# Entrance of the experts: token weights, slot weights, activation table and unread products moved or dropped

## The chip, the cores and the metric

The kernel runs on one core of a Trainium2 chip. The core has five engines with queues of their own, which are worked off in the order written: TensorE (PE in the profile, its weight loads PEld), VectorE (DVE), ScalarE (ACT), GpSimd (POOL) and SyncE (SP), and 16 DMA engines. The metric is the time of one execution in microseconds (us), lower is better: 1363.2 us is the median of three runs (1360.3 to 1363.39).

## The reference

The program is an encoder trunk with two layers on 512 tokens of width 1024. Each layer has a mixer (two kinds of attention) and a mixture of 16 experts, of which every token uses two. What matters here is the second part:

```python
scores = jax.nn.sigmoid((t @ w_router).astype(jnp.float32))
sel = scores + router_bias.astype(jnp.float32)
...
_, idx = lax.top_k(jnp.where(in_group, sel, -jnp.inf), TOP_K)
top_s = jnp.take_along_axis(scores, idx, axis=-1)
gate = top_s / jnp.sum(top_s, -1, keepdims=True)
...
act = jax.nn.silu(hg) * hu * combine[..., None].astype(t.dtype)
y = jnp.einsum('tef,efd->td', act, w_down)
```

The router picks one of four groups of experts and two experts in it; `gate` is the weight of each chosen expert for a token, and an expert's hidden activation is multiplied by it.

## The kernel before, in words

Each expert has 128 slots (`CAP`). The kernel does not run every expert on every token: it computes for each slot of an expert the number of the token that sits there (`tidx`), gathers these rows of `h2d` from DRAM with an indirect DMA of GpSimd (`x_load`, tile `xe`), transposes them on TensorE (`x_split`, tile `tp`), and splits them into a high and a low part (`xH` by ScalarE, `xL` by VectorE). The weights of gate, up and a half of down are split in the same way: ScalarE casts 512 columns into `wH` (line 217), VectorE subtracts into `wL` (line 218); there are six buffers of each (`NWH`). A product is then three matmuls (lines 227 to 229): high by high, low by high, high by low. An expert takes 24 of them for gate (8 blocks of 128 channels), 24 for up, and 8 wider ones for down.

The stage between the router and the first expert, which is called the entrance here, runs once per layer:

- VectorE ranks the scores, and TensorE counts the places (`pos`, lines 1068 to 1071). VectorE turns places into eight one-hot tiles `ats` (line 1088), TensorE multiplies them into `mp` (line 1090), and VectorE reads `tidx` out of it (line 1100).
- Behind `mp` TensorE has seven products of 512 columns into `idle` (line 1096), which nothing reads.
- GpSimd gathers the rows of the first expert. Then every engine loads the largest count `cnti` (line 1229) and branches: if an expert had more than 128 tokens, a loop (`overflow`) would handle the rest. It is not taken with these inputs. Instructions written behind the branch cannot be issued ahead of it, and a buffer that the branch would use is only free when the engine that would use it has passed its own branch.
- Behind the branch come the casts and subtractions of expert 0's weights, the transposes of its rows, and its products. `token_weights` (lines 1106 to 1111: six small VectorE operations, with the copy `posf`) gives each token the weights of its two experts. `slot_weights` (lines 1117 to 1121) turns them to the order of slots: ScalarE converts `ats` to 32 bits (`atf`, 1024 columns), TensorE multiplies it with the weights (`gp`, eight products of 16 columns, two instructions each in the profile), VectorE copies `gp` to `gsl`. The first reader of `gsl` is the end of expert 0's up product (line 1166).
- ScalarE loads its table of functions twice here: at its first cast behind the branch (line 217) and at the first Silu (line 1159).

What order the engines work in is decided when the program is built: a scheduler places instructions by their dependences, and `tc.issue_after(z.ins)` holds instructions back behind the one named. Behind the entrance the experts run in a steady cycle, e + 1's rows being split while e's down product runs. Experts' weights come in by SyncE's DMA queue, 1 MB per transfer; the first seven are loaded ahead, five more wait for the first gather (`load_held`, a one-column ScalarE copy at line 1311).

Of the kernel before, what the change touches and what calls it, by code (L numbers as in the profile page):

```python
# [12 lines left out]
AF = mybir.ActivationFunctionType  # L13
# [5 lines left out]
P = 128  # L19
S = 512  # L20
D = 1024
NT = S // P
# [62 lines left out]
def build(tc, A, out):  # L85
    nc = tc.nc
    with ExitStack() as es:
# [11 lines left out]
        V, ACT, PE, PO, SY = nc.vector, nc.scalar, nc.tensor, nc.gpsimd, nc.sync  # L99

        def f4(name, shape, dt=F32):
            return fp.tile([P] + list(shape), dt, tag="f4", name=name)
# [4 lines left out]
        def sc(name, shape, dt=F32, p=P):  # L107
            return sp.tile([p] + list(shape), dt, tag="sc", name=name)

        def small(name, shape, dt=F32, bufs=4, p=P):  # L110
            return sm.tile([p] + list(shape), dt, tag=name, name=name, bufs=bufs)
# [4 lines left out]
        def ptp(shape, name="tp", dt=F32):  # L116
            return ps.tile(shape, dt, tag="tp", name=name, bufs=2)

        def pat(shape, name="at"):
            return ps.tile(shape, F32, tag="at", name=name, bufs=4)  # L120
# [19 lines left out]
        for n in ("ident", "enc", "mhalf"):  # L140
            o, w = _COLS[n]
            t = cst.tile([P, w], F32, name="c_" + n)
# [9 lines left out]
        oneb = cst.tile([P, P], BF16, name="oneb")  # L152
# [27 lines left out]
        issued = {}  # L180
# [152 lines left out]
        def turn(dst, src):  # L333
            k = src.shape[0]
            return PE.transpose(dst, src, ident[0:k, 0:k])  # L335

        def transposes(src, dst, n):
            for i in range(n):
                turn(dst[:, i, :], src(i))

        def split_ps(p, H, L):
            ACT.copy(H, p)  # L342
            return V.tensor_sub(L, p, H.bitcast(F32))  # L343
# [79 lines left out]
        def layer(l, hH, hL, W0, after=None, qk=None):  # L423
# [21 lines left out]
            for j in range(2):  # L445
                g = gq[:, j, :]
                V.tensor_mul(t1[:, j], cosv, g[:, None, :].to_broadcast([P, NT, HD]))
                gp = g.rearrange("p (d two) -> p d two", two=2)
# [222 lines left out]
            for i in range(len(units) + LAG):  # L671
# [4 lines left out]
                if i >= LAG:  # L676
                    h, t = units[i - LAG]
# [163 lines left out]
            last = ACT.activation(nm, nm, AF.Exp)  # L841
# [207 lines left out]
            v4s, at = g4(sel), 0  # L1049
# [24 lines left out]
            src = sc("src", [2 * NT, 2, NE], BF16)  # L1074
# [8 lines left out]
            mp = pat([P, NE], "mp")  # L1083
            ats = f4("ats", [2 * NT, P], BF16)
            for k in range(2):
                for t in range(NT):
                    at = ats[:, NT * k + t]
                    V.tensor_scalar(at, iotab, sv[:, 0, k, t:t + 1], None, op0=OP.is_equal)
                    for i in range(2):
                        last = PE.matmul(mp, lhsT=at, rhs=src[:, NT * k + t, i], start=(k == 0 and t == 0 and i == 0),  # L1090
                                         stop=(k == 1 and t == NT - 1 and i == 1))
            with tc.issue_after(last.ins):

                idle = pat([P, 512], "idle")
                for i in range(NIDLE):
                    warm = PE.matmul(idle, lhsT=oneb, rhs=ats[:, 0:4], start=(i == 0), stop=(i == NIDLE - 1))
            cnti = small("cnti", [1], I32, bufs=1)
            V.tensor_reduce(cnti, pos[:, NT, :], axis=X, op=OP.max)
            tidx = small("tidx", [NE], I32, bufs=1)
            order1 = V.tensor_scalar(tidx, mp, -1.0, float(S), op0=OP.mult, op1=OP.add)  # L1100

            gsl, posf = rt("gsl", [NE]), rt("posf", [NT + 1, NE])

            def token_weights():

                V.tensor_mul(tmp, o12, sco[:, None].to_broadcast([P, 2, NT, NE]))
                V.reduce_sum(sv[:, 1], tmp, axis=X)
                den = rt("den", [NT])
                V.tensor_add(den, sv[:, 1, 0, :], sv[:, 1, 1, :])
                V.reciprocal(den, den)  # L1110
                V.tensor_mul(tmp, tmp, den[:, None, :, None].to_broadcast([P, 2, NT, NE]))

            def slot_weights():

                gp = pat([P, NE], "gp")
                atf = f4("atf", [2 * NT, P])
                ACT.copy(atf, ats)
                for n in range(2 * NT):
                    PE.matmul(gp, lhsT=atf[:, n], rhs=tmp[:, n // NT, n % NT], start=(n == 0), stop=(n == 2 * NT - 1))
                V.tensor_copy(posf, pos)  # L1120
                V.tensor_copy(gsl, gp)

            r_g2 = row_load(moddr[l, 5])

# [4 lines left out]
            def x_load(e):  # L1129

                xe = xes[e % len(xes)]
                XE[e] = xe
                return PO.indirect_dma_start(
                    out=xe, out_offset=None, in_=h2d,
                    in_offset=bass.IndirectOffsetOnAxis(ap=tidx[:, e:e + 1], axis=0),
                    bounds_check=S - 1, oob_is_err=False)

            def x_split(e):
                xe = XE.pop(e)
                xH = f4("xH", [8, P], F32R)  # L1140
                xL = f4("xL", [8, P], F32R)
                for q in range(2):
                    p = ptp([P, 4, P])
                    transposes(lambda i: xe[:, (4 * q + i) * P:(4 * q + i + 1) * P], p, 4)
                    i = split_ps(p, xH[:, 4 * q:4 * q + 4, :], xL[:, 4 * q:4 * q + 4, :])
                XS[e] = xH, xL
                return i
# [8 lines left out]
            def x_gate(e):  # L1156
                p = x_prod(e, "gate")
                a = sc("ea", [256])
                ACT.activation(a, p, AF.Silu)
                WD[e] = a  # L1160
# [66 lines left out]
            def overflow():  # L1227
# [1 line left out]
                rv = nc.values_load(cnti[0:1, 0:1], min_val=0, max_val=S,  # L1229
                                    skip_runtime_bounds_check_because="a count of tokens")  # L1230
                with tc.If(rv > CAP):
                    token_weights()
                    row = rt("row", [2, NT])
                    V.tensor_scalar(row, sv[:, 0], float(CAP), None, op0=OP.is_ge)
                    code = rt("code", [NT])
# [68 lines left out]
            def load_held():  # L1304

                hold = None
                for e, w, tag in AHEADW[HOLD:]:
                    with ExitStack() as order:
                        if hold is not None:
                            order.enter_context(tc.issue_after(hold.ins))  # L1310
                        PRE[e, w] = wraw(x_src(e, w), x_shape(w), tag, first=None if hold else lambda z: ACT.copy(z, XE[0][:, 0:1]))
                    hold = hold or issued["load"]

            overflow()
            load_held()
            with tc.issue_after(warm.ins):
                split0 = x_split(0)
            for e in range(NE):
                if e + AHEAD < NE:
                    x_load(e + AHEAD)  # L1320
                if e == EKEEP:
                    keep_weights()
                x_gate(e)
                if e == 0:
                    with tc.issue_after(split0.ins):
                        token_weights()
                        slot_weights()
                if e > 0:
                    x_down(e - 1)
                x_up(e)  # L1330
                if e + 1 < NE:
                    x_split(e + 1)
# [49 lines left out]
        for l in range(DEPTH):  # L1382
            h = layer(l, *h)
# [3 lines left out]
NXE = 3  # L1387
BEHIND = ((0, "gate"), (0, "up"))
HOLD = 7
NIDLE = 7  # L1390
DS = ((0, 1), (1, 1))
WPAT = ("e8",) * 5 + ("raw",) * 4
NE8 = 5
# [35 lines left out]
```

## Time and profile before

| what | value |
|---|---|
| median of three runs | 1363.2 us |
| the profiled execution's own time | 1365.39 us |
| its span in the profile | 1363.6 us |
| TensorE busy | 1269.8 us (93%) |
| VectorE busy | 1015.7 us (74%) |
| ScalarE busy | 712.3 us (52%) |
| mean granted clock of TensorE | 0.975 |
| entrance of layer 0 | 492 to 500 us, expert 0 to 510 us |
| entrance of layer 1 | 1154 to 1162 us, expert 0 to 1172 us |

A row of the timeline names the start, the duration of the group, the engine, the line, the operation, out<-in, shapes and count; in square brackets stands how long the engine had been idle and what ended that. The chain that ended last is followed back from the last instruction, at each step to what released it. PEclk and the clock column are the granted clock of TensorE as a share of full speed: 1.00 is 2.4 GHz, 0.50 is 1.2 GHz. Instructions that stand in a merged row overlap, so a row's duration over its count is a little above their spacing.

### The profile page before, as it was taken

Reading aid. Unit: us, or ns where it says so; the run is one execution under the profiler, and the core shown is the slowest. Engines: PE = TensorE matmul, PEld = TensorE weight load, DVE = VectorE, ACT = ScalarE, POOL = GpSimd, SP = SyncE. Lnnn points to the kernel's source line nnn. Section 1 sums busy time; section 2 is a strip of 40 time slices with the busy share of each in tenths; the row PEclk is TensorE's granted clock in tenths of the full one; section 3 lists DMA queues with packets and bytes.
Section 4 is the critical chain, followed back from the end, with each engine's and each line's share of the span. In section 5 each row is a group of like instructions: output and inputs, shape, how many; then the busy total and the mean of one; then the engine's idle time right before and its main releaser. Section 6 shows DMA issues by size and latency. Waiting matters only on the chain.

```text
span 1363.6 us, 21396 instructions
## 1 busy us (share of the span) xinstructions
PE 1269.8 (93%) x7967; PEld 1031.1 (76%) x7971; DVE 1015.7 (74%) x2064; ACT 712.3 (52%) x1476; POOL 145.5 (11%) x122
## 2 busy tenths in 40 slices
PE   5899999999999959999889999999999995899997
PEld 4788777778778948888658777777777795788883
DVE  5888778766378879999587887564235878799986
ACT  2344444554744157777445445456555513777770
POOL 1031000000000012222111300000000001223210
PEclk9999999999999969999989999999999997999999
DMA  9745555346165178999553455121214534889963
GB/s 319 230 140 169 185 186 184 126 155 210 38 201 217 63 276 327 313 342 330 177 186 129 155 186 186 63 62 63 63 47 141 192 131 171 322 300 352 335 187 153
DMA packets 124221, 259.37 MB, mean 190 GB/s; under 512 B 18009, under 2 KB 67577, under 8 KB 116176
## 3 DMA queue, kind: packets, MB, share of 16 engines
q1 hardware_dynamic: 102672, 225.46, 46.6%
q0 software_dynamic: 9184, 15.69, 4.9%
q10 hardware_dynamic: 12256, 16.80, 3.9%
q8 instruction: 64, 1.05, 0.3%
q14 instruction: 45, 0.37, 0.1%
HBM read 246.57 MB, written 27.30 MB: 201 GB/s over the span
## 4 chain that ended last, share of the span: by engine, by line
PE 39%; DVE 14%; ACT 4%; DMA 3%; issue 3%; POOL 1%; SPq 0%; ACTq 0%; POOLq 0%; DVEq 0%
DVE wL L218 8%; PE mm L229 6%; PE mm L228 6%; PE mm L227 6%; PE mm L1203 6%; PE tp L335 3%; PE y L1343 2%; PE av L664 1%; ACT wH L217 1%; DMA xr<-xdr 1%; PE y L1360 1%; DMA raw<-in_w_in 1%; ACT eT L1186 1%; DMA xe<-h2d,tidx 1%; DVE ea L1166 1%
## 5 line engine op out<-in xcount | busy, mean ns | idle before, releaser
L218 DVE TENSOR_TENSOR wL<-raw,wH 128x512 fp32r<-128x512 f32 x520 | 340.4, 686 | 95.5 <-ACT wH L217 85.1
L217 ACT CAST wH<-raw 128x512 fp32r<-128x512 f32 x520 | 318.8, 622 | 159.6 <-PE mm L1203 45.7
L227 PE MATMUL mm<-hH,wH 128*128 128x512 f32 x544 | 218.8, 402 | 0.0
L228 PE MATMUL mm<-hL,wH 128*128 128x512 f32 x544 | 216.9, 399 | 0.0
L229 PE MATMUL mm<-hH,wL 128*128 128x512 f32 x544 | 215.8, 397 | 0.0
L227 PE MATMUL mm<-wH,xH 128*128 128x256 f32 x512 | 148.0, 289 | 0.5 <-ACT xH L342 0.5
L229 PE MATMUL mm<-wH,xL 128*128 128x256 f32 x512 | 147.0, 288 | 0.5 <-DVE xL L343 0.5
L228 PE MATMUL mm<-wL,xH 128*128 128x256 f32 x512 | 145.7, 285 | 0.5 <-DVE wL L218 0.5
L228 PEld LDWEIGHTS mm<-hL,wH 128*128 128x128 f32 x544 | 103.0, 189 | 21.6 <-issue 1.8
L227 PEld LDWEIGHTS mm<-hH,wH 128*128 128x128 f32 x544 | 103.0, 189 | 21.5 <-issue 0.8
L229 PEld LDWEIGHTS mm<-hH,wL 128*128 128x128 f32 x544 | 103.0, 189 | 21.2 <-issue 0.7
L251 DVE SCALAR_TENSOR_TENSOR acc<-araw,cond,acc 128x512 f32<-128x512 f32 x148 | 110.6, 748 | 4.7 <-DMA araw<-in_w_ada 1.9
L227 PEld LDWEIGHTS mm<-wH,xH 128*128 128x128 f32 x512 | 98.1, 192 | 2.6 <-ACT xH L342 1.4
L228 PEld LDWEIGHTS mm<-wL,xH 128*128 128x128 f32 x512 | 98.1, 192 | 2.1 <-DVE wL L218 0.9
L229 PEld LDWEIGHTS mm<-wH,xL 128*128 128x128 f32 x512 | 97.4, 191 | 1.4 <-DVE xL L343 0.9
L1208 POOL DMA_INDIRECT xsum<-ye,tidx x28 | 50.4, 1800 | 214.8 <-DVE wL L218 116.8
L288 POOL TENSOR_TENSOR rstd<-rstd,c_mhalf 128x1 f32<-128x1 f32 x32 | 19.6, 614 | 490.0 <-DVE rstd L287 475.3
L638 ACT ACTIVATE pp<-s,nm,rs 128x512 f32<-128x512 f32 x64 | 49.7, 778 | 33.3 <-DVE nm L635 30.9
L1203 PE MATMUL mm<-raw,eT 128*128 128x512 f32 x128 | 63.3, 617 | 3.7 <-ACT eT L1186 1.6
L227 PE MATMUL mm<-wH,hH 128*128 128x256 f32 x192 | 56.9, 299 | 7.1 <-ACT hH L407 4.3
L229 PE MATMUL mm<-wH,hL 128*128 128x256 f32 x192 | 55.4, 295 | 1.9 <-DVE hL L377 0.9
L228 PE MATMUL mm<-wL,hH 128*128 128x256 f32 x192 | 55.0, 290 | 0.0
(299 smaller groups left out, 2637.6 us busy)
## 6 DMA issues: line engine op xcount, KB each, us to landing
araw<-in_w_ada SPq DMA_DIRECT2D x44, 1024.0 KB
raw<-in_w_in SPq DMA_DIRECT2D x40, 1024.0 KB
raw<-in_w_exp_gate SPq DMA_DIRECT2D x32, 1024.0 KB
raw<-in_w_exp_up SPq DMA_DIRECT2D x30, 1024.0 KB
raw<-in_w_exp_down SPq DMA_DIRECT2D x28, 1024.0 KB
raw<-in_w_out SPq DMA_DIRECT2D x8, 1024.0 KB
eraw<-in_w_ada SPq DMA_DIRECT2D x4, 1024.0 KB
raw<-in_w_branch_a SPq DMA_DIRECT2D x4, 1024.0 KB
```

The lines of the kernel that those rows point to most:

```text
L217: ACT.copy(H, raw(s))
L218: V.tensor_sub(L, raw(s), H.bitcast(F32))
L227: PE.matmul(o, lhsT=lH, rhs=rH, start=(i == 0), stop=False)
L228: PE.matmul(o, lhsT=lH, rhs=rL, start=False, stop=False)
L229: PE.matmul(o, lhsT=lL, rhs=rH, start=False, stop=(i == n - 1))
L251: last = V.scalar_tensor_tensor(acc, raw[:, k, :], ck, acc, op0=OP.mult, op1=OP.add)
L288: PO.tensor_tensor(r, r, mhalf[:, :n], op=OP.pow)
L335: return PE.transpose(dst, src, ident[0:k, 0:k])
L638: ACT.activation(pp, s, AF.Exp, bias=nm, scale=rs, accum_out=dn)
L1203: PE.matmul(p, lhsT=a, rhs=w, start=(i == 0), stop=(i == len(todo) - 1))
L1208: PO.indirect_dma_start(out=xsum, out_offset=bass.IndirectOffsetOnAxis(ap=tidx[:, e:e + 1], axis=0), in_=ye, in_offset=None, bounds_check= ...
L1343: PE.matmul(Y[t][j], lhsT=G[:, i, t, :], rhs=YE[i][:, 512 * j:512 * j + 512], start=start, stop=stop)
```

## The change

The token weights are computed ahead of the branch instead of behind it, in the main path alone (the branch reads them). The conversion `atf` and a one-column Silu stand ahead of the first split; the Silu, which reads `mp`, makes ScalarE load its table ahead of the branch, and the two loads behind it fall away. The slot weights' products are held behind the last of expert 0's transposes (`turn0`) and no longer wait for the token weights behind `xL`. `gsl` is copied by ScalarE. The seven products into `idle` are gone, and with them the order that held the first transposes behind them.

```diff
--- before.py
+++ after.py
@@ -336,7 +336,7 @@
 
         def transposes(src, dst, n):
             for i in range(n):
-                turn(dst[:, i, :], src(i))
+                issued["turn"] = turn(dst[:, i, :], src(i))
 
         def split_ps(p, H, L):
             ACT.copy(H, p)
@@ -1087,13 +1087,8 @@
                     at = ats[:, NT * k + t]
                     V.tensor_scalar(at, iotab, sv[:, 0, k, t:t + 1], None, op0=OP.is_equal)
                     for i in range(2):
-                        last = PE.matmul(mp, lhsT=at, rhs=src[:, NT * k + t, i], start=(k == 0 and t == 0 and i == 0),
-                                         stop=(k == 1 and t == NT - 1 and i == 1))
-            with tc.issue_after(last.ins):
-
-                idle = pat([P, 512], "idle")
-                for i in range(NIDLE):
-                    warm = PE.matmul(idle, lhsT=oneb, rhs=ats[:, 0:4], start=(i == 0), stop=(i == NIDLE - 1))
+                        PE.matmul(mp, lhsT=at, rhs=src[:, NT * k + t, i], start=(k == 0 and t == 0 and i == 0),
+                                  stop=(k == 1 and t == NT - 1 and i == 1))
             cnti = small("cnti", [1], I32, bufs=1)
             V.tensor_reduce(cnti, pos[:, NT, :], axis=X, op=OP.max)
             tidx = small("tidx", [NE], I32, bufs=1)
@@ -1113,12 +1108,13 @@
             def slot_weights():
 
                 gp = pat([P, NE], "gp")
-                atf = f4("atf", [2 * NT, P])
-                ACT.copy(atf, ats)
                 for n in range(2 * NT):
                     PE.matmul(gp, lhsT=atf[:, n], rhs=tmp[:, n // NT, n % NT], start=(n == 0), stop=(n == 2 * NT - 1))
+                ACT.copy(gsl, gp)
+
+            with tc.issue_after(order1.ins):
+                token_weights()
                 V.tensor_copy(posf, pos)
-                V.tensor_copy(gsl, gp)
 
             r_g2 = row_load(moddr[l, 5])
 
@@ -1229,7 +1225,6 @@
                 rv = nc.values_load(cnti[0:1, 0:1], min_val=0, max_val=S,
                                     skip_runtime_bounds_check_because="a count of tokens")
                 with tc.If(rv > CAP):
-                    token_weights()
                     row = rt("row", [2, NT])
                     V.tensor_scalar(row, sv[:, 0], float(CAP), None, op0=OP.is_ge)
                     code = rt("code", [NT])
@@ -1313,8 +1308,11 @@
 
             overflow()
             load_held()
-            with tc.issue_after(warm.ins):
-                split0 = x_split(0)
+            atf = f4("atf", [2 * NT, P])
+            ACT.activation(small("tbl", [1], bufs=1), mp[:, 0:1], AF.Silu)
+            ACT.copy(atf, ats)
+            x_split(0)
+            turn0 = issued["turn"]
             for e in range(NE):
                 if e + AHEAD < NE:
                     x_load(e + AHEAD)
@@ -1322,8 +1320,7 @@
                     keep_weights()
                 x_gate(e)
                 if e == 0:
-                    with tc.issue_after(split0.ins):
-                        token_weights()
+                    with tc.issue_after(turn0.ins):
                         slot_weights()
                 if e > 0:
                     x_down(e - 1)
@@ -1387,7 +1384,6 @@
 NXE = 3
 BEHIND = ((0, "gate"), (0, "up"))
 HOLD = 7
-NIDLE = 7
 DS = ((0, 1), (1, 1))
 WPAT = ("e8",) * 5 + ("raw",) * 4
 NE8 = 5
```

TensorE's queue behind the branch (`tp` are the transposes of expert 0's rows `xe`, `gp` the slot weights, `mm` the products of gate and up; "-" is before, "+" is after):

```order
 L335 MATMUL tp<-c_ident,xe 128x128 x8
-L227 MATMUL mm<-wH,xH 128x256
-L228 MATMUL mm<-wL,xH 128x256
+L1112 MATMUL gp<-rt_tmp,atf 128x16 x4
+L227 MATMUL mm<-wH,xH 128x256
+L228 MATMUL mm<-wL,xH 128x256
+L1112 MATMUL gp<-rt_tmp,atf 128x16 x4
 L227 MATMUL mm<-wH,xH 128x256
 L228 MATMUL mm<-wL,xH 128x256
...
 L227 MATMUL mm<-wH,xH 128x256
-L1119 MATMUL gp<-rt_tmp,atf 128x16 x8
 L228 MATMUL mm<-wL,xH 128x256
```

All 16 instructions of `gp` moved from the middle of the up product, some 33 products behind the transposes, to right behind the transposes, with two products of 256 columns between the halves. The seven products into `idle`, six ahead of the branch and one behind it, are gone from the queue.

ScalarE's queue behind the branch, before (`wH` are casts of weights, the copy to `raw` releases the held transfers, `xH` are expert 0's rows, `ea` is the Silu):

```order
L217 ACT_TABLE_LOAD
L217 CAST wH<-raw 128x512 x6
L1311 COPY raw_5091<-xe 128x1
L342 CAST xH<-tp 128x512 x2
L1117 CAST atf<-ats 128x1024
L217 CAST wH<-raw 128x512 x3
L1159 ACT_TABLE_LOAD
L1159 ACTIVATE ea<-mm 128x256
L217 CAST wH<-raw 128x512 x4
L342 CAST xH<-tp 128x512 x2
```

Of these, the two loads, `atf` and three of the first six casts stand elsewhere in the same place after:

```order
L1313 CAST atf<-ats 128x1024
L217 CAST wH<-raw 128x512 x3
L1306 COPY raw_5084<-xe 128x1
L217 CAST wH<-raw 128x512 x2
L342 CAST xH<-tp 128x512 x2
L217 CAST wH<-raw 128x512
L1113 COPY rt_gsl<-gp 128x16
L217 CAST wH<-raw 128x512 x3
L1155 ACTIVATE ea<-mm 128x256
L217 CAST wH<-raw 128x512 x5
L342 CAST xH<-tp 128x512 x2
```

Both table loads left this place (one stands ahead of the branch now), `atf` moved to the head, three casts instead of six stand ahead of the copy that waits for the gather, two of them between it and `xH`, and the copy of `gsl` is new here.

VectorE's queue behind the branch, after (`wL` are the subtractions, `xL` those of the rows, first of expert 0 and then of expert 1, `ea` the end of expert 0's up product):

```order
L218 TENSOR_TENSOR wL<-raw,wH 128x512 x5
L343 TENSOR_TENSOR xL<-tp,xH 128x512 x2
L218 TENSOR_TENSOR wL<-raw,wH 128x512 x7
L1162 SCALAR_TENSOR_TENSOR ea<-ea,rt_gsl,mm 128x256
L218 TENSOR_TENSOR wL<-raw,wH 128x512 x2
L343 TENSOR_TENSOR xL<-tp,xH 128x512 x2
```

Before, six, three, two and one `wL` stood in the four places, with the token weights among the three and the copy of `gsl` behind them: 12 `wL` ahead of expert 1's `xL`, and now 14, two of them between `ea` and `xL` instead of one. On SyncE's queue one transfer of expert 5's down weights moved from ahead of the five held ones to behind them.

## Rows read from the trace of the kernel before

**Rows 1.** The page's head line, the span of the execution:
```profile
span 1363.6 us, 21396 instructions
```

**Rows 2.** Busy by stretch: length, PE, PEld, DVE, ACT, POOL, then clock, DMA share, GB/s:
```profile
480.00:484.00 4.00, 1.86 (x8) 1.78 (x9) 3.30 (x5) 0.00 (x0) 0.67 (x1) 0.50 1.02 230
503.00:504.00 1.00, 1.00 (x9) 1.00 (x9) 1.00 (x4) 0.91 (x2) 0.89 (x1) 0.85 1.02 389
1159.00:1160.00 1.00, 0.00 (x0) 0.00 (x0) 0.65 (x2) 1.00 (x3) 0.77 (x1) 1.00 0.41 78
1162.00:1163.00 1.00, 0.90 (x5) 0.93 (x6) 0.00 (x0) 0.18 (x1) 0.00 (x0) 0.53 0.69 242
1166.00:1168.00 2.00, 2.00 (x19) 2.00 (x18) 1.52 (x5) 1.79 (x4) 0.00 (x0) 1.00 1.00 383
```

**Rows 3.** The chain that ended last, layer 1: start us, us, what:
```profile
1156.04 0.19 DVE tidx L1100
1157.03 4.94 DMA xe<-h2d,tidx
1162.11 1.94 PE tp L335 x8
1164.05 0.40 PE mm L227
1164.66 0.21 PE mm L227
1166.51 0.12 PE mm L227
1168.95 1.93 PE gp L1119 x16
...
1200.57 2.69 PE mm L1203 x7
1210.93 2.69 PE mm L1203 x7
```

**Rows 4.** Timeline at the entrance, layer 1, TensorE and ScalarE:
```profile
1156.23 2.34 PE L1096 MATMUL idle<-ats,oneb 128*128 128x512 bf16 x5 [0.23 <-issue]
1158.70 2.18 ACT L217 CAST wH<-raw 128x512 fp32r<-128x512 f32 x4 [1.30 <-PEq L1231]
1163.23 0.58 ACT L342 CAST xH<-tp 128x512 fp32r<-128x512 f32 x1 [1.05 <-PE tp L335]
1164.56 1.05 ACT L1117 CAST atf<-ats 128x1024 f32<-128x1024 bf16 x1
1167.90 1.28 ACT L1159 ACT_TABLE_LOAD   x1
```

**Rows 5.** Timeline at the entrance, layer 1, VectorE:
```profile
1165.31 0.28 DVE L1106 TENSOR_TENSOR rt_tmp<-rt_o,rt_sco 128x128 f32<-128x128 f32 x1
1168.53 0.28 DVE L1111 TENSOR_TENSOR rt_tmp<-rt_tmp,rt_den 128x128 f32<-128x128 f32 x1
1170.92 0.17 DVE L1121 COPY rt_gsl<-gp 128x16 f32<-128x16 f32 x1 [2.11 <-PE gp L1119]
1173.09 0.69 DVE L218 TENSOR_TENSOR wL<-raw,wH 128x512 fp32r<-128x512 f32 x1
```

**Rows 6.** Timeline of TensorE, eight router products at either clock level:
```profile
476.97 1.07 PE L985 MATMUL lg<-wrt,x1T 128*128 128x16 f32 x8 [0.60 <-ACT x1T L979]
479.97 1.89 PE L985 MATMUL lg<-wrt,x1T 128*128 128x16 f32 x8 [0.68 <-ACT x1T L979]
```

**Rows 7.** Timeline of TensorE early in the kernel:
```profile
22.90 5.18 PE L335 MATMUL tp<-c_ident,x 128*128 128x128 f32 x20
28.01 2.21 PE L265 MATMUL adap<-cond,araw 128*64 128x1 f32 x36
43.55 0.41 PE L227 MATMUL mm<-wH,hH 128*128 128x256 f32 x1
49.31 0.29 PE L227 MATMUL mm<-wH,hH 128*128 128x256 f32 x1
```


## The prediction

> **What bounds the kernel now.** I read the clock and busy times by stretch first, then the chain of waits, then the timeline of each engine at the entrance of layer 1; layer 0 has the same instructions 662 us earlier. From VectorE's `tidx` the chain goes to the gather of the first expert's rows, which takes 4.94 us, and to the eight transposes at 1162.11; from there on it is TensorE alone to the end of expert 0's up product [rows 3]. So two things set the end of this stage: when the gather lands, and how fast TensorE gets through 8 transposes, 48 products of 256 columns and 16 narrow instructions of the slot weights (`gp`). What the other engines do between 1156 and 1162 lies beside the gather.
>
> The speed of TensorE is not constant here. At 1159 to 1160, with TensorE idle, the granted clock is 1.00; when the transposes come it is 0.53, and only from 1166 it is 1.00 again; in layer 0 it comes back within 503 to 504 [rows 2]. The steps of the chain show the price: a product of 256 columns steps by 0.21 us at the lower level and 0.12 at the higher [rows 3]. Between the transposes and the rise the engine did the transposes and some eight of these wide products.
>
> Behind the entrance an expert takes 10.36 us from one down product to the next (1210.93 less 1200.57, rows 3), in a closed ring of all three engines through six weight buffers. A delay of TensorE at the entrance therefore goes into the end, unless VectorE has a lead that saves a later wait.
>
> **The change part by part, per layer.**
>
> The unread products: seven on TensorE, five of which take 2.34 us in a row [rows 4]. They run while the gather is under way, and TensorE then stands idle until 1162.11. They hold back TensorE's branch, and with it ScalarE's third cast by 1.30 us [rows 4]. Both lie beside the gather: 0 gained. Did they hold the clock for the transposes? In the rows it was up behind them and down again when the transposes began [rows 2], so nothing is lost either; were there executions where it lasts, before would be quicker there by up to the price of the low stretch, 16 products of 0.21 instead of 0.12 or 1.4 us.
>
> Token weights: six VectorE operations from 1165.31 to 1168.53, of at most 0.28 us each [rows 5], so under 1.7 us, go to the time ahead of the branch. That delays VectorE's branch and its first `wL`; the gather's remaining 4.9 us covers it. GpSimd's first gather stands ahead of its branch and waits for `tidx` alone, which is not moved: the gather lands as before, 0.
>
> Table loads: the one behind the branch and the one of 1.28 us at 1167.90 [rows 4] become one, which runs while ScalarE waits for `mp`. Hidden before too, since ScalarE's Silu is read long after: 0. `atf`, 1.05 us [rows 4], now stands ahead of the first cast; only three casts are done when the gather lands instead of six, and two stand between the copy and `xH`. The first `xH` started at 1163.23 [rows 4]; behind two casts of 0.55 us (four took 2.18, rows 4) it starts some 0.15 later. Cover: the first half of `gp` on TensorE. Without it the 0.15 would be on the path.
>
> The held transfers: the down weights of expert 5 move behind five others on SyncE's queue. They are wanted some 50 us later: 0.
>
> Slot weights: the 16 instructions of `gp` took 1.93 us at the higher level [rows 3]. They now run right behind the transposes, at the lower level. The same form, a 128x128 weight load with 16 columns, shows both prices: eight take 1.07 us at 476.97 and 1.89 us at 479.97, where the clock is 0.50 [rows 6, 2]. If the clock rose at the same moment as before, this would cost nothing: narrow and wide instructions step almost alike, so the ones in the low stretch would only change places. But then the two wide products between the halves are all that the engine does besides transposes and narrow work for 16 steps. Rows of this kernel show such a stretch: early on, 20 transposes in 5.18 us and 36 one-column products in 2.21 us follow each other closely, and yet the product at 43.55 still takes 0.41 us, the long form of the lower level, against 0.29 at 49.31 [rows 7]. So I take it that the clock here rises as far behind the wide products as before, and that all 16 run at the lower level: 2 x (1.89 - 1.07) = +1.64 us. Bounds: 0, if it rises when it did; 1.64 + 1.44 = +3.1, if the low stretch comes once more (16 products at 0.21 instead of 0.12).
>
> The Trainium skill weighs this otherwise: "TensorE: Matmul & The Clock Gate", Part 1, says that the warm-up is a matter of time and not of the number of matmuls. By that rule the term is 0 and the second rival below stands; by the early rows it is 1.64.
>
> Waits that go: TensorE no longer waits for `xH` (the step of 0.40 at 1164.05 against 0.21, rows 3): -0.19. VectorE's 2.11 us wait for `gp` [rows 5] goes, but TensorE was running through it.
>
> What is late next: with `wH` buffers given back later, VectorE's queue has two `wL` between `ea` and expert 1's `xL` where it had one, at 0.69 us [rows 5]: TensorE's first product that reads `xL` is +0.69 late. Against it VectorE is then two `wL` further, 1.38 less the 0.69, and I let this lead pay the 0.69 back in experts 1 and 2: -0.69. Bounds of the two together: -0.69 to +0.69.
>
> Sum: 1.64 - 0.19 + 0.69 - 0.69 = +1.45 us per layer, +2.9 in two. The profiled execution's own time is 1365.39, its span 1363.6 [rows 1] and 1.8 around it; so 1368.3 against it. The median of the runs shown, 1363.2, lies 2.2 below that execution: 1366.1.
>
> **The rivals.** The clock rises when it did (the skill's rule). For it: here it rose three to four microseconds behind the first transpose [rows 3], with transposes for half of that time. Then the layer is worth -0.19, with VectorE's lead -0.88; in two layers -0.4 to -1.8, so 1361.4 to 1362.8, say 1362.2.
>
> A second low stretch, which ends slower than before: narrow work fills the time in which the clock rose, and the level stays low for as long again behind `gp`. Place: expert 0's gate and up products. Price 1.44 more per layer, 1366.1 + 2.9 = 1369.0. It decides from about seven more wide products at the lower level than I forecast (7 x 0.09 = 0.6 us per layer, which brings the change over 4.1 us). For it: the early rows. Against it: 46 wide products stand in a row behind `gp`.
>
> VectorE was the real limit: its 2.11 us wait and the token weights (under 1.7) leave its queue, 3.5 us per layer after all, 1363.2 - 7.0 = 1356.2. For it: `wL` stands in the chain of every expert. Against it: TensorE stepped without a pause from 1162.11 to the end of up, so VectorE's wait was beside it, and six buffers let VectorE run ahead little.
>
> **How the numbers follow.** Forecast 0.50, clock as before 0.30, second low stretch 0.13, VectorE 0.07. The forecast's own range is 1363.5 to 1368.5. To hold 8 in 10 the range takes in the second case and most of the third: 1360.5 to 1369.5. About 0.3%, 4.1 us, is what a measurement of this kernel can tell from no change: 1359.1 and 1367.3. Slower: 0.2 of the forecast's chance (0.10) and 0.85 of the third case (0.11), 0.21. Faster: most of the last (0.06) and a little of the second (0.02), 0.08. Same: 0.71.
>
> **What would show it.** Right: `gp` behind the transposes with eight in about 1.9 us, products of 256 columns at the long form until some 6.6 us behind the first transpose, TensorE's last up product some 1.4 us later behind the first transpose than before, no wait for `xH`, two `wL` between `ea` and `xL`. Gather, its landing and ScalarE's single load should be as told. Wrong: a clock of 1.00 within 3.5 us of the first transpose (second case), steps of 0.21 beyond 8 us (third), a gather that starts at another distance from `tidx`, or a cycle of the experts other than 10.36 us.

## The result, and the profile after

After: 1371.05 us, median of 20 runs (1363.15 to 1377.09). Before, on the same chip: 1362.56 us, median of 20 (1355.94 to 1369.52). The ratio is 1.0058, 95% interval 1.0042 to 1.0075, some 7.9 us slower. The forecast was 1366.1, at most 1369.5, and "same" the likeliest; the change is slower.

The profiled execution took 1371.44 us against 1365.39 before, so it shows 6.05 us of the loss. The span in the profile is 1369.7 us, against 1363.6 in [rows 1], and the mean granted clock 0.966, against 0.975.

TensorE at the entrance of layer 1 in the timeline (start, busy us, engine, line, operation, idle time before and what ended it); the counterparts are in [rows 3]:

```profile
1165.46 1.94 PE L335 MATMUL tp<-c_ident,xe 128*128 128x128 f32 x8 [5.67 <-DMA xe<-h2d,tidx]
1167.19 1.73 PE L1112 MATMUL gp<-rt_tmp,atf 128*128 128x16 f32 x8
1168.76 0.56 PE L227 MATMUL mm<-wH,xH 128*128 128x256 f32 x1
...
1169.33 1.72 PE L1112 MATMUL gp<-rt_tmp,atf 128*128 128x16 f32 x8
1170.89 0.56 PE L227 MATMUL mm<-wH,xH 128*128 128x256 f32 x1
...
1174.03 0.30 PE L229 MATMUL mm<-wH,xL 128*128 128x256 f32 x1
...
1177.88 1.03 PE L335 MATMUL tp<-c_ident,xe 128*128 128x128 f32 x8
...
1180.51 0.39 PE L229 MATMUL mm<-wH,xL 128*128 128x256 f32 x1 [0.77 <-DVE xL L343]
```

TensorE never pauses from 1165.46 to the second expert's transposes at 1177.88, yet its products keep the long step of 0.21 until the one at 1174.03, 8.6 us behind the first transpose. Before, the first shorter one came at 1165.31, 3.2 us behind it, and in layer 0 at 503.19, 3.0 us behind it. The rows of before, with the wait for the second expert's `xL` in layer 1:

```profile
503.19 0.34 PE L227 MATMUL mm<-wH,xH 128*128 128x256 f32 x1
1165.31 0.36 PE L228 MATMUL mm<-wL,xH 128*128 128x256 f32 x1
1174.49 0.39 PE L229 MATMUL mm<-wH,xL 128*128 128x256 f32 x1 [0.23 <-DVE xL L343]
```

In layer 0 of the kernel after the first shorter one stands at 511.87, 10.9 us behind the first transpose:

```profile
500.96 1.94 PE L335 MATMUL tp<-c_ident,xe 128*128 128x128 f32 x8 [5.98 <-DMA xe<-h2d,tidx]
...
506.75 0.42 PE L228 MATMUL mm<-wL,xH 128*128 128x256 f32 x1
...
511.23 0.42 PE L228 MATMUL mm<-wL,xH 128*128 128x256 f32 x1
511.44 0.60 PE L229 MATMUL mm<-wH,xL 128*128 128x256 f32 x2
511.87 0.30 PE L227 MATMUL mm<-wH,xH 128*128 128x256 f32 x1
```

The granted clock by stretch (stretch, its length, TensorE's busy time and instructions, clock, DMA share, GB/s) says the same; [rows 2] had 0.85 at 503 and 1.00 from 1166:

```profile
503.00:504.00 1.00, 1.00 (x6) 0.50 0.93 360
511.00:512.00 1.00, 1.00 (x7) 0.56 0.95 397
1166.00:1168.00 2.00, 2.00 (x12) 0.50 0.77 240
1173.00:1174.00 1.00, 1.00 (x6) 0.50 1.05 430
1174.00:1175.00 1.00, 1.00 (x10) 0.97 1.03 426
```

Two stretches hold the whole loss of the profiled execution. Between the first transpose and the second expert's transposes: 13.43 and 12.42 us in layers 0 and 1, before 10.26 and 10.38, together 5.21. From there to the first down product: 6.21 and 6.27, before 5.63 and 5.64, together 1.21; that is the wait for `xL`, 0.72 and 0.77 where it was 0.23, and 0.08 more for `xH`, 0.32 where it was 0.24. The gather is not part of it in this pair of executions: from `tidx` to the first transpose 5.95 and 5.63, before 5.47 and 6.07, sums within 0.04.

### The profile page after: what moved, and what is told of

Its sections match the earlier page's. It is cut to its first block, busy times and chain, and to the rows that moved or that the text cites. A ratio compares the mean times of both kernels' runs of the same rounds, so it can differ in the third digit from the quotient of the medians.

```text
span 1369.7 us, 21369 instructions
## 1 busy us (share of the span) xinstructions
PE 1264.3 (92%) x7957; PEld 1030.1 (75%) x7957; DVE 1015.9 (74%) x2062; ACT 709.9 (52%) x1478; POOL 148.3 (11%) x122
## 4 chain that ended last, share of the span: by engine, by line
PE 61%; DVE 22%; DMA 6%; ACT 5%; issue 3%; POOL 2%; ACTq 0%; SPq 0%; POOLq 0%; DVEq 0%
DVE wL L218 10%; PE mm L227 10%; PE mm L228 10%; PE mm L229 10%; PE mm L1199 6%; PE tp L335 4%; PE av L664 3%; PE y L1340 2%; ACT wH L217 2%; POOL rs L288 1%; PE s L630 1%; PE s L631 1%; DVE acc L251 1%; PE pa L228 1%; PE pa L227 1%
```

## Experiments

Theory A: the narrow products (`gp`) right behind the transposes keep the clock at its lower level. Theory B: the unread products had lifted it, and they are gone. Theory C: the order of casts on ScalarE makes `xL` late. Each kernel's stretches come from the starts in its timeline, layer 0 / layer 1. The ratio is to before on the same chip.

| kernel | ratio (95%) | tidx to first transpose | first to second transposes | from there to down |
|---|---|---|---|---|
| before | 1 | 5.47 / 6.07 | 10.26 / 10.38 | 5.63 / 5.64 |
| after | 1.0058 (1.0042 to 1.0075) | 5.95 / 5.63 | 13.43 / 12.42 | 6.21 / 6.27 |
| e1 gp behind gate | 1.0023 (0.9998 to 1.0048) | 6.46 / 5.48 | 10.15 / 10.78 | 6.11 / 6.10 |
| e2 before, no unread | 1.0010 (0.9994 to 1.0027) | 5.55 / 6.12 | 10.13 / 10.08 | 5.62 / 5.62 |
| e3 after, with unread | 1.0029 (1.0012 to 1.0046) | 6.36 / 5.68 | 13.09 / 12.38 | 6.10 / 6.11 |
| e4 gp ahead | 0.9996 (0.9978 to 1.0015) | 6.67 / 5.72 | 9.66 / 9.47 | 5.71 / 5.70 |
| e5 gsl on VectorE | 1.0054 (1.0027 to 1.0081) | 6.56 / 5.63 | 12.45 / 12.36 | 6.25 / 6.26 |
| e6 16 wide ahead | 1.0010 (0.9991 to 1.0028) | 6.83 / 5.65 | 11.53 / 8.45 | 6.11 / 6.11 |
| e7 16 wide, gp behind gate | 1.0019 (1.0002 to 1.0036) | 6.52 / 5.75 | 15.55 / 9.70 | 5.84 / 6.11 |
| e8 gp behind wide | 1.0004 (0.9988 to 1.0021) | 6.08 / 5.61 | 9.14 / 7.65 | 5.72 / 5.72 |
| e9 24 wide ahead | 1.0014 (0.9998 to 1.0031) | 5.94 / 5.55 | 8.45 / 8.45 | 6.27 / 6.26 |
| e10 wide behind tidx | 0.9989 (0.9967 to 1.0011) | 8.07 / 8.06 | 9.15 / 9.06 | 5.72 / 5.71 |
| e11 five behind gp | 1.0010 (0.9992 to 1.0027) | 9.26 / 6.53 | 8.58 / 8.09 | 6.11 / 6.11 |
| e12 atf behind xH | 1.0019 (0.9996 to 1.0042) | 6.42 / 5.67 | 10.56 / 10.92 | 6.11 / 6.10 |

The stretches belong to one execution. What lies outside them varies more than they do: from layer 0's first down product to layer 1's first `ats`, where these kernels are alike, 638.25 us in before, 637.52 in after, 630.42 in e1, 638.89 in e8. So causes are read from the stretches, and the ratio says what is left over all executions.

**e1: gp behind the gate product.**

```diff
-                    with tc.issue_after(turn0.ins):
+                    with tc.issue_after(issued["mm"].ins):
                         slot_weights()
...
```

Here `issued["mm"]` is the gate product's last matmul.

> The kernel after, with one thing put back: the slot weights' 16 narrow products stand behind the gate product's last matmul instead of right behind the transposes. Theory A (narrow products right behind the transposes keep the granted clock at its lower level): the clock is back at 1.00 some 3 to 6 us behind the first transpose in both layers, against 10.8 and 8.8 us in the kernel after; the time falls by about 5.5 us (3.29 + 2.22, the two layers' longer way from the first transpose to ea) to some 1365. Theory B (the clock is low because the unread products are gone): the low stretches stay at 9 to 11 us and the time at 1371. Theory C (the order of casts on ScalarE and VectorE): the wait of expert 1's first product that reads xL stays, 0.45 us per layer, so 0.9 us of the loss remain under A too.

Measured: 1365.68 us. TensorE's timeline in layer 0, and the wait for `xL`:

```profile
501.38 1.94 PE L335 MATMUL tp<-c_ident,xe 128*128 128x128 f32 x8 [6.49 <-DMA xe<-h2d,tidx]
...
504.80 0.30 PE L229 MATMUL mm<-wH,xL 128*128 128x256 f32 x1
...
514.01 0.38 PE L229 MATMUL mm<-wH,xL 128*128 128x256 f32 x1 [0.62 <-DVE xL L343]
```

The long steps end 3.4 us behind the first transpose (4.9 in layer 1), with no unread product ahead of them: A. The 0.62 us wait for `xL` stays, as C says (0.45 more per layer was expected, 0.39 it is).

**e2 and e3: the unread products alone.** e2 is before without its seven; e3 is after with them where before had them. The cut shows e2; e3 adds the same lines to after.

```diff
-            with tc.issue_after(last.ins):
-                idle = pat([P, 512], "idle")
-                for i in range(NIDLE):
-                    warm = PE.matmul(idle, lhsT=oneb, rhs=ats[:, 0:4], ...)
...
```

> The kernel before, with one thing taken away: the seven unread products ahead of the branch. Theory A: the clock comes back 3 to 4 us behind the first transpose as before, and the time stays within 1 us of before, at 1362 to 1364. Theory B: without them the clock stays low for 9 to 11 us behind the first transpose and the time rises by 5 to 8 us, to 1368 to 1371.

> The kernel after, with the seven unread products put back where they stood. Theory A: the time stays that of after, 1370 to 1372, with the clock low for 9 to 11 us behind the first transpose. Theory B: the low stretch is 3 to 4 us again, and the time falls by 5 to 8 us, to 1363 to 1366.

Measured: 1364.90 and 1370.14 us. In e2 (first) the level rises as before; in e3 (second) the unread products run, and the long steps last 10.1 us all the same:

```profile
503.10 1.94 PE L335 MATMUL tp<-c_ident,xe 128*128 128x128 f32 x8 [5.59 <-DMA xe<-h2d,tidx]
...
506.40 0.31 PE L229 MATMUL mm<-wH,xL 128*128 128x256 f32 x1
```

```profile
496.31 2.76 PE L1096 MATMUL idle<-ats,oneb 128*128 128x512 bf16 x6 [0.23 <-DVE tidx L1100]
502.47 1.94 PE L335 MATMUL tp<-c_ident,xe 128*128 128x128 f32 x8 [3.40 <-DMA xe<-h2d,tidx]
504.20 3.43 PE L1117 MATMUL gp<-rt_tmp,atf 128*128 128x16 f32 x16
...
512.52 0.32 PE L229 MATMUL mm<-wH,xL 128*128 128x256 f32 x1
```

B falls as the cause in these executions. e3's ratio, 1.0029, lies below after's 1.0058 (the plain quotient of its medians, 1370.14 and 1364.11, is 1.0044): whether the unread products spare part of the loss in others stays open.

The other kernels' traces leave A without an exception. Where `gp` stands right behind transposes at the lower level (after, e3 and e5, six entrances), the first shorter product comes 8.35 to 10.91 us behind the first transpose. Where wide products stand behind transposes at that level (before, e1, e2, e4, e10 and e12 in both layers, e11 in layer 0, thirteen entrances), it comes 3.00 to 5.86 us behind it.

**e4: gp ahead of the transposes.**

```diff
-            x_split(0)
+            slot_weights()
+            with tc.issue_after(issued["gp"].ins):
+                x_split(0)
...
```

> The kernel after, with the slot weights' 16 narrow products ahead of the transposes, in the time in which TensorE waits for the gather. Theory A: behind the transposes come wide products only, the clock is back 3 to 4 us behind the first transpose, the 16 products (1.9 us at the higher level, 3.8 at the lower) lie beside the gather and leave the path: first transpose to the end of expert 0's up product 1.9 us shorter than before, so 1362.6 - 3.8 + 0.9 (the wait for xL that Theory C keeps) = 1359.7. Theory B: the clock stays low as long as in after, only the 3.0 us of the narrow products leave the path in each layer: 1371 - 6 = 1365.

Measured: 1363.48 us. TensorE in layer 1:

```profile
1158.34 3.60 PE L1112 MATMUL gp<-rt_tmp,atf 128*128 128x16 f32 x16 [2.25 <-ACT atf L1313]
1161.84 1.94 PE L335 MATMUL tp<-c_ident,xe 128*128 128x128 f32 x8
...
1166.96 0.32 PE L227 MATMUL mm<-wH,xH 128*128 128x256 f32 x1
```

`gp` is off the path, but the long steps last 5.1 us behind the first transpose (5.9 in layer 0), not the 3 to 4 expected. Of the 1.9 us that the stretch was to lose against before, it loses 0.60 and 0.91: a miss of A's number, in the direction of A. In the time no difference from before is shown, and the 1359.7 of theory A was missed by 3.8 us.

**e5: gsl back on VectorE.**

```diff
-                ACT.copy(gsl, gp)
+                V.tensor_copy(gsl, gp)
```

> The kernel after, with one thing put back: the copy of the slot weights out of PSUM (gsl) is done by VectorE again, not by ScalarE. Theory C1 (the copy stands in ScalarE's queue ahead of casts and waits there for gp, so the casts and VectorE's wL behind them come late): expert 1's first product that reads xL waits 0.23 us in both layers as before, instead of 0.72 and 0.77 in after; the low stretch stays at 8 to 11 us; the time 1370, 0.9 below after. Theory C2 (atf ahead of the first casts, or two wL between ea and xL, make it late): the wait stays at 0.6 to 0.8.

Measured: 1371.62 us, and the wait is as long as in after, so C1 falls. The long steps last 8.56 and 8.35 us, with `gp` where after has it:

```profile
1179.80 0.38 PE L229 MATMUL mm<-wH,xL 128*128 128x256 f32 x1 [0.77 <-DVE xL L343]
```

**e6 and e9: wide work up to the transposes, gp behind them as in after.** 16 unread products in e6, as shown, 24 in e9.

```diff
+            with tc.issue_after(order1.ins):
+                for i in range(16):
+                    warm = PE.matmul(idle, lhsT=oneb, rhs=ats[:, 0:4], ...)
...
-            x_split(0)
+            with tc.issue_after(warm.ins):
+                x_split(0)
```

> The kernel after, with 16 unread products of 512 columns in the time in which TensorE waits for the gather, up to the first transpose; the slot weights' narrow products right behind the transposes as in after. Theory A1 (narrow products only keep the clock from rising): the transposes begin at 1.00 and everything behind them runs at 1.00; from the first transpose to the second expert's transposes 1.03 + 1.9 + 48 x 0.12 = 8.7 us plus the waits for xH, say 9.0, against 13.43 and 12.42 in after; the time 1363. Theory A2 (narrow products also bring the clock down): the transposes run at 1.00, and steps of 0.21 come back behind gp; 10.5 to 12.5 us per layer, the time 1366 to 1370. Theory D (the unread products hold up the branch and with it the casts, or the transposes): the first transpose is later behind the gather's landing, or a wait for xH of over 1 us stands behind it; the time 1370 or more.

> The kernel after with 24 unread products of 512 columns ahead of the first transpose instead of the 16 of the run before, so that TensorE has nearly no pause between them and the transposes in layer 0 too. Theory A2 (the level falls where a pause and then narrow products follow each other; without the pause it holds): no step of 0.21 behind the transposes in either layer, 8.5 us from the first transpose to the second expert's transposes in both (8.45 in layer 1 with 16); if the transposes come no later than the gather allows, 1364.3 - 1.9 x 2 = 1360.5; each us by which the last unread product outlasts the gather is added. Rival A3 (narrow products bring the level down, pause or not): steps of 0.21 come back behind gp in at least one layer, 11 to 12 us there, the time 1366 or more.

Measured: 1365.66 and 1366.78 us. e6 has both cases in one execution:

```profile
503.76 1.06 PE L335 MATMUL tp<-c_ident,xe 128*128 128x128 f32 x8 [3.01 <-DMA xe<-h2d,tidx]
504.66 3.05 PE L1112 MATMUL gp<-rt_tmp,atf 128*128 128x16 f32 x16
...
511.75 0.36 PE L228 MATMUL mm<-wL,xH 128*128 128x256 f32 x1
...
1166.49 1.06 PE L335 MATMUL tp<-c_ident,xe 128*128 128x128 f32 x8 [0.99 <-DMA xe<-h2d,tidx]
1167.39 1.86 PE L1112 MATMUL gp<-rt_tmp,atf 128*128 128x16 f32 x16
```

In layer 0 the unread products end 3.0 us ahead of the transposes: these still run at the higher level (1.06 us for eight, against 1.94), but inside `gp` it goes, and the wide products step by 0.21 up to 511.75. In layer 1, with 0.99 us of pause, nothing falls. The clock of e6 (columns: length, busy time of PE, PEld, DVE, ACT, POOL, then clock, DMA share, GB/s):

```profile
504.00:505.00 1.00, 1.00 (x12) 1.00 (x10) 0.60 (x1) 0.93 (x3) 0.00 (x0) 1.00 0.94 221
505.00:507.00 2.00, 2.00 (x12) 2.00 (x11) 1.33 (x3) 0.50 (x2) 0.99 (x1) 0.52 0.78 301
1168.00:1174.00 6.00, 6.00 (x53) 6.00 (x53) 4.98 (x9) 4.82 (x11) 0.99 (x1) 1.00 0.97 365
```

e9 leaves 0.48 us of pause in layer 0 and none in layer 1, and `gp` passes at the higher level in both:

```profile
504.24 1.06 PE L335 MATMUL tp<-c_ident,xe 128*128 128x128 f32 x8 [0.48 <-DMA xe<-h2d,tidx]
505.14 1.86 PE L1112 MATMUL gp<-rt_tmp,atf 128*128 128x16 f32 x16
```

So A2: the same 16 narrow products cost 1.9 us where the level is up when they come and 3.4 where it is down (e3's row), and they do not by themselves bring it down. A3 falls, and a fall with narrow work left out comes below (e7, e8). The clock's part of the loss is undone, 8.45 us in both layers, and still e9 is not faster than before: A's time missed by 6 us. Two terms of it are known. The unread products stand among the slots' products (`mp`), and `tidx` comes 2.56 us behind the first `ats` instead of 1.71; and the wait for `xL` adds 0.6. Together 1.5 of the 1.9 us per layer; the rest stays open.

**e7, e8, e10, e11: a version faster than before?** e7: e6's wide work with `gp` behind the gate and `gsl` on VectorE. e8: `gp` behind unread products, all ahead of the transposes; it has twelve of these, not the sixteen that its expectation speaks of, and the trace has all twelve ahead of `gp`. e10 and e11: the same with the unread products reading `posf`, so that they come behind `tidx`, eight ahead of `gp` and two (five) behind it. The cut shows e10, where `wide(n)` issues n unread products.

```diff
+                wide(8)
...
+                        issued["gp"] = PE.matmul(gp, lhsT=atf[:, n], ...)
...
+                wide(2)
...
```

> The kernel after, with the slot weights behind the gate product's last matmul, their copy on VectorE, and the 16 unread products of 512 columns up to the first transpose. Theory A: the clock is at 1.00 from the first transpose on, 9.0 us from there to the second expert's transposes against 10.26 and 10.38 in before, the wait for xL 0.23 as before: 1364.1 - 2.6 = 1361.5. Theory D (the unread products hold up the casts or the transposes): 1364 or more, with a longer wait for xH or xL.

> The kernel after with the slot weights' 16 narrow products ahead of the transposes, among 16 unread products of 512 columns that start behind the slots' product. Theory A: wide work up to the transposes lifts the clock before them, and gp is off the path: from the first transpose to the second expert's transposes 1.03 + 48 x 0.12 and waits for casts of 0.3 to 1.0, so 7.1 to 7.8 us against 10.3 in before; the time 1364.3 - 2 x 2.5 = 1359.3. Theory D (the unread products hold TensorE's branch, and so the casts, or outlast the gather): waits for xH, wH or xL of over 1.5 us behind the transposes and a time of 1363 or more.

> The kernel after with gp ahead of the transposes as before in this study, eight unread products of 480 columns ahead of it and two behind it; their columns are read from posf, which VectorE writes behind tidx, so none of them can stand among the slots' products (mp). Theory A with the delay of tidx as the term that ate the gain of the last two kernels: tidx 1.71 us behind the first ats again (2.55 with the unread products among mp), the first transpose 5.5 to 6.5 behind tidx, 7.7 to 9.2 from there to the second expert's transposes against 10.26 and 10.38, and 5.7 from there to the first down product; 1.2 to 2.6 us less than before per layer, so 1360 to 1362.5 where before has 1364.5. Rival D (the unread products hold TensorE's branch and with it the casts, or outlast the gather): over 6.8 us from tidx to the first transpose, or waits for casts of over 1.5 us, and 1364 or more.

> The same with five unread products behind gp instead of two, which bridge more of the pause ahead of the transposes. Theory A: no step of 0.21 behind the transposes in either layer, 7.7 us to the second expert's transposes, 1360 to 1361.5. Rival D: the three more products come while the gather has landed (the level still low ahead of gp), the first transpose is up to 1.2 us later in each layer, and the time is that of the kernel with two or up to 2 us more.

Measured: 1365.94, 1365.11, 1362.67 and 1365.86 us; none is shown to beat before. Each lost its gain elsewhere. In e7 the casts came late (TensorE waits 0.50 for `wH` behind the transposes), the level fell in layer 0, and `gp` at the gate's end prolonged the low stretch to 519.98. e8 has the shortest stretch of all, 7.65 in layer 1, pays 0.84 in `tidx` in each layer, and loses the level in layer 0:

```profile
503.09 1.06 PE L335 MATMUL tp<-c_ident,xe 128*128 128x128 f32 x8 [1.33 <-DMA xe<-h2d,tidx]
...
505.54 0.42 PE L228 MATMUL mm<-wL,xH 128*128 128x256 f32 x1
```

Here and in e7's layer 0 the transposes still ran at the higher level, wide products alone stood behind them, and the steps of 0.21 came all the same. So narrow work right behind the transposes is not needed for the fall: in e6 it was at hand, and that it was the cause is not shown. The pauses ahead of the transposes were 3.01, 2.67 and 1.33 us in the three entrances that lost the level, and 1.21 or less in those that kept it (both layers of e9, layer 1 of e6, e7, e8 and e11); whether the pause alone decides is not shown.

e10 shows why such a version is a gamble:

```profile
1153.67 3.66 PE L1114 MATMUL idle<-rt_posf,oneb 128*128 128x480 bf16 x8 [0.62 <-DVE rt_posf L1129]
1157.13 3.43 PE L1122 MATMUL gp<-rt_tmp,atf 128*128 128x16 f32 x16
1160.40 0.96 PE L1114 MATMUL idle<-rt_posf,oneb 128*128 128x480 bf16 x2
1161.15 1.91 PE L335 MATMUL tp<-c_ident,xe 128*128 128x128 f32 x8
```

The level did not rise behind the eight wide products, so `gp` took 3.43 us and the transposes waited for TensorE, 8.06 us behind `tidx`. In e11's layer 1 it did rise, and the same 16 took 1.85:

```profile
1161.98 1.85 PE L1122 MATMUL gp<-rt_tmp,atf 128*128 128x16 f32 x16
```

**e12: atf back behind the xH casts, on top of e1.**

```diff
-            ACT.copy(atf, ats)
-            x_split(0)
...
+            split0 = x_split(0)
+            with tc.issue_after(split0.ins):
+                ACT.copy(atf, ats)
```

> The kernel after with the slot weights behind the gate product and, beyond the first run of this study, the cast atf back behind expert 0's two xH casts, where before has it. Theory C2 (atf ahead of the first casts makes them late, and VectorE with them): the wait of expert 1's first product that reads xL is 0.23 us as before, and 5.6 us lie between the second expert's transposes and the first down product, against 6.1 with atf ahead; the time 1364 to 1365. Theory C3 (there is one weight cast more ahead of expert 1's xH on ScalarE, fourteen where before has thirteen, and behind it one wL more ahead of xL): the wait stays at about 0.6 and the stretch at 6.1.

Measured: 1365.38 us, and the wait stands, so C2 falls too:

```profile
513.27 0.38 PE L229 MATMUL mm<-wH,xL 128*128 128x256 f32 x1 [0.62 <-DVE xL L343]
```

C3 agrees, but was not tried alone; e4 has fourteen casts as well and waits 0.22 to 0.23. In after the rows show VectorE's order: two `wL` behind `ea`, then `xL` ([rows 5] had one):

```profile
1178.18 0.47 DVE L1162 SCALAR_TENSOR_TENSOR ea<-ea,rt_gsl,mm 128x256 f32<-128x256 f32 x1
1178.57 1.29 DVE L218 TENSOR_TENSOR wL<-raw,wH 128x512 fp32r<-128x512 f32 x2
1179.77 1.28 DVE L343 TENSOR_TENSOR xL<-tp,xH 128x512 fp32r<-128x512 f32 x2
```

In e12 it is one `wL`, and `ea` itself is late. What makes VectorE late by 0.5 us in all kernels with the change's order but e4, e8 and e10 stays open.

## Why the prediction was wrong

The failing step is the one on the slot weights: "I take it that the clock here rises as far behind the wide products as before". It does not. The long steps were to end some 6.6 us behind the first transpose; they ended 10.9 and 8.6 us behind it, beyond the 8 us that were to show the third rival. Before, six and seven wide products ran before the short steps came, the half-way one included; in after 28 and 17 did. That is 22 and 10 more at 0.213 (22 steps from 506.75 to 511.44 in layer 0) instead of 0.12, 2.05 and 0.93 us. Their mean, 1.49, is the price of the third rival (1.44 per layer), and both layers pass the seven from which it was to decide. That rival, with a chance of 0.13, is what happened in kind: with `gp` right behind transposes at the lower level the rise was put off, and e1, which only moves `gp`, has it 3.4 and 4.9 us behind the first transpose again. That the mean of the two layers meets 1.44 so closely is partly luck, as 2.05 and 0.93 lie far apart.

- The price of `gp`, +1.64 from the `lg` rows, and no wait for `xH` behind the first transposes, -0.19: +1.45 together, measured some 1.15. Between wide products the 16 take 3.13 us (from 504.61 to 506.39 in layer 0 less a step of 0.21, twice) against 1.99 before. The first of the two was right in kind and too large. The second wait is gone, as told, but brought nothing by itself: the first wide product behind each half of `gp` takes the same 0.40 in the chain that was read as that wait. With the late rise this makes 3.20 and 2.08 us, for 3.17 and 2.04 measured. The chain of after in layer 0 (start, us, what):

```profile
502.90 1.52 PE gp L1112 x8
504.42 0.40 PE mm L227
504.82 0.21 PE mm L228
505.03 1.52 PE gp L1112 x8
506.55 0.40 PE mm L227
```

- The clock as before (the second rival): not seen in either layer, and e1 to e3 show that the place of `gp` made the difference. The Trainium skill, "TensorE: Matmul & The Clock Gate", Part 1, on which it leaned, makes warm-up a matter of time and not of the number of matmuls, and says that the count varies from run to run; here TensorE was busy without a pause from the first transpose on, and the rise took 10.9 and 8.6 us, against 3.0 and 3.2 before. The trace disagrees: it was not the time alone.
- Two `wL` ahead of `xL`, +0.69: they came as told, and the wait grew by 0.49 and 0.54. That they are its cause is not shown: e1 and e12 have one `wL` there and still wait 0.61 to 0.62. VectorE's lead, -0.69, did not pay the wait back: the first down product is later by the whole wait, and behind it the experts run as before (185.55 us from layer 1's first down product to the end, before 185.47). So this pair is worth +1.1 to 1.2 us in two layers where the sum had 0, the second step that failed; e5 and e12 say that neither `gsl` nor `atf` on ScalarE is its cause alone.
- Unread products, worth 0: right by e2 (1.0010, interval across 1). They were not worth keeping, and where they stand among the slots' products they cost 0.84 us of `tidx` (e6 to e9).
- Token weights, tables and held transfers, 0: after's own stretches do not contradict it; the sum from `tidx` to the first transpose is 11.58 against 11.54. But between the layers it shifted, +0.48 and -0.44, as in most kernels with the change's order, and in e1, e3, e5 and e12 the sum is 11.94 to 12.19, so a loss of 0.4 to 0.65 us in other executions is not excluded. The reason stays open.
- The early rows of [rows 7], which spoke for the forecast and the third rival: weaker than told. Between the narrow work and the product at 43.55 TensorE paused for 2.31 and 0.98 us, and the clock column of before says 1.00 for that stretch, so that only the step tells the level there.
- VectorE as the real limit: wrong, as its freed wait for `gp` brought nothing.

The sum by measured terms is 5.21 + 1.21 + 0.04 = 6.5 us, against 6.05 between the two profiled executions and some 7.9 by the ratio; the forecast had 2.9. The third rival stood at 1369.0, within the range, because it was priced with `xL` paid back; with the 1.2 us it is 1370.2. What the median of 1371.05 has beyond that is not traced to a stretch.

## What to carry to other kernels

Ahead of moving small products to where an engine "is waiting anyway", look at the clock of that stretch. At the lower level they are dearer themselves (3.4 us for the 16 instead of 1.9), and right behind the transposes they put off the rise for everything behind them. In these traces it paid to have wide products first behind the pause and the narrow ones behind the rise (before, e1, e2). Filling the pause with unread wide work kept the level in both layers only in e9, and what it then delayed took most of the gain: none of these versions is shown to beat before.

## What the runs showed of the hardware

- The granted clock stayed at its lower level for over 10 us while TensorE was busy all the time (after, layer 0), with transposes, 16 narrow products and 28 wide ones. With the wide ones right behind the transposes the first shorter product came 3.0 to 5.1 us behind the first transpose (before, e1, e2, e12).
- The same 16 narrow products right behind the transposes let the level stand at 1.00 (e9, both layers) or saw it fall (e6, layer 0); the two differ in the pause ahead of the transposes, 0.48 us and none against 3.01. The level also fell behind the transposes with wide products alone, after a pause of 1.33 us (e8, layer 0) and of 2.67 (e7, layer 0).
- Eight products of 480 columns in a row lifted the level in one layer of e11 and in none of e10: the same instructions, 3.43 us or 1.85 us of `gp` behind them. When it rises is not set by the instructions alone.
- Executions of one kernel lie 6 to 16 us apart (1361.72 to 1367.77 in e2, 1359.44 to 1375.87 in e1), as much as the whole effect of the change or more.
